# Stick-breaking attention with a woven output projection: value products sent for two steps at a time

## The chip, the cores and the metric

One core of a Trainium2 chip runs the whole program in one launch. The metric is device time in microseconds (us), the median of several runs of the same kernel. A profiled execution is a run of its own; its trace gives times from the start of its span.

## What is computed

One layer of a streaming encoder: an input projection, stick-breaking attention with 8 heads of 64 (2,048 new frames, and 8 running streams with 16 frames each over 1,024 cached ones), an HGRN2 recurrence with 4 heads of 128, an output projection and a LayerNorm. The parts that matter here, cut from the reference:

```python
def stick_breaking_attention(q, k, v, q_offset):
    z = jnp.einsum('bhqd,bhkd->bhqk', qblk, kf) * scale
    mask = kpos[None, :] < qpos[:, None]
    log_keep = jnp.where(mask, jax.nn.log_sigmoid(-z), 0.0)
    later = lax.cumsum(log_keep, axis=3, reverse=True) - log_keep
    w = jnp.where(mask, jnp.exp(jax.nn.log_sigmoid(z) + later), 0.0)
    return jnp.einsum('bhqk,bhkd->bhqd', w, vf)
...
    mixed = jnp.concatenate([o_sb, o_hg], axis=-1).astype(x.dtype)
    out = jnp.einsum('bte,ed->btd', mixed, w_out)
    y = layer_norm(DEEPNORM_ALPHA * x + out, ln_g, ln_b)
```

So per head: scores, two sigmoids of them (the weight and what is kept), a running product along the keys, and the product with the values.

## The kernel before

The program has three stages on one timeline. First come the input projection and the HGRN2 chunks (to about 1,000 us). Then the attention over the prompt runs in 160 **units**, and a second stream of work is woven between them. Last comes what is left of the output projection.

A unit is one pair of heads, one block of 128 queries and up to 512 keys (`CW`); 64 query blocks times head pairs are cut into 160 units, from the last keys to the first. The first unit of a block holds the diagonal and is 1 to 4 blocks of 128 keys wide, all others are 4 wide. A unit goes through four parts, written in `run_steps` (L1000) as a software pipeline over steps n:

- `z_part(n + 3)`, L721: the scores of both heads, one PSUM bank each (`pz`, two banks in all). Each matmul has 64 rows, and the two heads sit on the two halves of the array (L734). In the first unit of a block a mask product (L731) goes ahead of them. ScalarE then makes `s` (L737) and `keep` (L740) from the scores. For units below 90 the `keep` of the second head is made by GpSimd from `s` instead (L742).
- `s_part(n + 2)`, L746: VectorE scans `keep` (L701) and GpSimd multiplies `s` by the result (L754).
- `t_part(n)`, L759: four transposes per head (L767) into one of two PSUM banks (`pw`), copied by ScalarE to `wh` (L107).
- `c_part(n - 1)`, L771: the value products (L783). They use 64 columns of the array per head and add up over the units of a block in one PSUM bank, `po`. After the last unit of a block VectorE multiplies them with the gate (L795), and after every second block a DMA stores the result to `mx_d`.

Within a step the order on TensorE is written out by hand:

```python
for i in range(2):
    run_later(); s_part(n + LS, i)
    if 0 <= n < NU: t_part(n, i)
    if i == 1:
        z_part(n + LZ); c_part(n - 1)
    tick()
    credit[0] += rate
    while credit[0] >= 1: next(guest, None); credit[0] -= 1
```

So a step is: transposes of head 0, guest, transposes of head 1, scores, value products, guest. The **guest** is a generator that sends one piece of other work each time it is called. For steps 0 to 89 it is the attention of the running streams (`all_samples`, L971). From step 90 on it is the output projection (`out_proj`, L1161, `out_first`, L1120), called 0.9 times per half step (`ORATE`). One of its pieces is two of the eight `e`, with three matmuls each of 512 columns (`py`, L1109 to L1111), so 6 matmuls. A 128-row block takes 48. A call can also find nothing to send: where the block's inputs are not there yet, where they are being split into two parts (L1104), or where a piece of the LayerNorm's tail is run. What the guest has not sent when the units end is sent afterwards without a break. TensorE takes its instructions in this order, and each engine waits on the others by semaphores.

Of the kernel before, what the change touches and what calls it, by code (L numbers as in the profile page):

```python
# [17 lines left out]
P = 128  # L18
# [10 lines left out]
LEVELS = (1, 2, 4, 8, 16, 32, 64)  # L29
BLK = 32  # L30
C0 = -2
W0 = 6
WL = 3
I0 = 2
PRE = 2
# [30 lines left out]
def stream_step_kernel(ctx: ExitStack, tc: tile.TileContext, x_prompt, x_sample, cache_k, cache_v, state_s,  # L66
# [83 lines left out]
                units.append((job, qb, lo, min(lo + CW, nk), lo + CW >= nk, lo == 0))  # L150
    NU = len(units)
    NS = 90
    SH0 = pool
    SH1 = dve
    KE = pool
# [517 lines left out]
    with ExitStack() as ph:  # L673
# [2 lines left out]
        qk = E("qk", 2)  # L676
        row = E("row", 2)
        fix = E("fix")
        wtp = E("wtp", 4)
        pz = E("pz", 2, space=PSUM)  # L680
        one = []
        smp_ctx = ExitStack()
# [88 lines left out]
        def c_part(u):  # L771
            if u < 0 or u >= NU:
                return
            job, qb, lo, hi, top, bot = units[u]
            p = jobs[job][0]
            if top:
                Os[p] = pa.tile([P, 512], F32, name="po", tag="po")
            o, v, n = Os[p], Vs[job], (hi - lo) // P
            th = [WT.pop((u, a)) for a in range(2)]
            for x in range(n):  # L780
                for a in range(2):
                    r = slice(a * DH, (a + 1) * DH)
                    mm(o[r, :P], v[:, lo // P + x, r], th[a][:, x * P:(x + 1) * P],  # L783
                       start=top and x == 0, stop=bot and x == n - 1)
            if bot:
                finish(p, qb)

        mos = {}

        def finish(p, qb):  # L790
            po, gt, e = Os.pop(p), Gs[(p, qb // 4)], qb % 2
            if e == 0:
                mos[p] = qk.tile([P, 2, P], F32, name="mo", tag="mo", bufs=3)
            mo = mos[p]
            later.append(lambda: dve.tensor_tensor(mo[:, e], po[:, :P], gt[:, qb % 4 * P:(qb % 4 + 1) * P], ALU.mult))  # L795

            def store():
                dma.dma_start(mx_d[p][:, (qb - 1) * P:(qb + 1) * P], mo)
                done.add((p, qb // 2))

            if e:
                defer(store, 4)
# [197 lines left out]
        def run_steps(n0, n1, guest, rate):  # L1000
            for n in range(n0, n1):
                for fn in todo.pop(n, []):
                    fn()
                for i in range(2):
                    run_later()
                    s_part(n + LS, i)
                    if 0 <= n < NU:
                        t_part(n, i)
                    if i == 1:
                        z_part(n + LZ)  # L1010
                        c_part(n - 1)
                    tick()
                    if n >= -LZ:
                        credit[0] += rate
                    while credit[0] >= 1:
                        next(guest, None)
                        credit[0] -= 1
# [10 lines left out]
        hg_ctx.close()  # L1028
        pw = E("pw", 2, space=PSUM)
        px = E("px", 2, space=PSUM)  # L1030
        pa = E("pa", 1, space=PSUM)
        one.append(E("pone", 1, space=PSUM).tile([P, 1], F32, name="one"))
        dve.memset(one[0], 1.0)
        sk = smp_ctx.enter_context(ALLOC("sk"))
# [85 lines left out]
        def out_first():  # L1120
            raw = {}

            def load(e):
                if e < KT:
                    raw[e] = io.tile([P, DM], F32, name="wor", tag="xr", bufs=3)
                    dma.dma_start(raw[e], w_out[0, e * P:(e + 1) * P, :])

            load(0)
            out_load(0)
            load(1)  # L1130
            for _ in range(W0):
                yield
            bs = io.tile([P, 2, 6], F32, name="bs", tag="bs")
            ps = [px.tile([P, 512], F32, name="py", tag="px") for _ in range(2)]
            for i in range(2 * KT + WL):
                e, c = divmod(i, 2)
                if e < KT:
                    if c == 0:
                        load(e + 2)
                    cs = slice(c * 512, c * 512 + 512)  # L1140
                    h, l, r = (t[:, cs] for t in (woh[:, e], wol[:, e], raw[e]))
                    eng = (dve, pool)[c]
                    copy(act, h, r)
                    later.append(lambda eng=eng, h=h, l=l, r=r: eng.tensor_tensor(l, r, f32(h), ALU.subtract))
                if i in (0, 2):
                    out_split(0, i // 2)
                if e == KT:
                    out_load(1)
                    out_x(0)
                if i >= WL:  # L1150
                    e, c = divmod(i - WL, 2)
                    cs = slice(c * 512, c * 512 + 512)
                    out_mm(0, ps[c], e, cs)
                    if e == KT - 1:
                        add(0, bs, c, cs, ps[c])
                yield
            dma.dma_start(lng, ln_g.to_broadcast([P, DM]))
            dma.dma_start(lnb, ln_b.to_broadcast([P, DM]))
            tails.extend(norm(BLKS[0], L[0]["x"], bs))

        def out_proj():  # L1161
            yield from out_first()
            for k, blk in list(enumerate(BLKS))[1:]:
                while k not in L:
                    out_load(k)
                    yield
                    yield
                for hf in range(2):
                    if hf not in L[k]:
                        out_split(k, hf)  # L1170
                        yield
                out_load(k + 1)
                while tails:
                    run_tail()
                    yield
                out_x(k)
                x = L[k]["x"]
                bs = io.tile([P, 2, 6], F32, name="bs", tag="bs")
                for c in range(2):
                    cs = slice(c * 512, (c + 1) * 512)  # L1180
                    ps = px.tile([P, 512], F32, name="py", tag="px")
                    for e in range(KT):
                        out_mm(k, ps, e, cs)
                        if e % 2 == 1:
                            if c == 1 and e % 4 == 3:
                                out_split(k + 1, e // 4)
                            run_tail()
                            out_load(k + 1)
                            out_x(k + 1)
                            yield  # L1190
                    add(k, bs, c, cs, ps)
                tails.extend(norm(blk, x, bs))
            while tails:
                run_tail()
                yield
# [3 lines left out]
        def run_tail():  # L1199
            if tails:  # L1200
                tails.pop(0)()
# [5 lines left out]
        def norm(blk, x, bs):  # L1207
# [28 lines left out]
            def both():  # L1236
# [1 line left out]
                shift(h1, SH1)  # L1238

            skip = lambda: None  # L1240
            return [skip, stats, skip, skip, lambda: center(h0, SH0), lambda: center(h1, SH1), both,
                    lambda: store(slice(0, DM))]

        guest = out_proj()
        run_steps(NS, NU + 1, guest, ORATE)
        run_later()
        run_later()
        run_later()
# [27 lines left out]
```

## Time and profile before

| what | value |
|---|---|
| median of 3 runs | 1751.0 us (1747.85 to 1751.8) |
| the profiled execution | 1749.85 us, of which the span is 1748.0 us |
| TensorE matmul, busy | 1707.1 us of the span (98%) |
| VectorE, ScalarE, GpSimd busy | 958.5, 701.2, 731.2 us |
| chain that ended last | 92% on TensorE |
| value products (L783) | 2,176 rows, 155.0 us busy |
| scores (L734) | 640 rows, 170.5 us busy |
| transposes (L767) | 1,088 rows, 171.5 us busy |

The profile is of one execution. Rows of matmuls overlap: the time that a group takes on TensorE is read from its start to the start of the next group, not from its length. A row of the timeline such as "x16" stands for so many instructions in a row. A float32 matmul of the scores and of the value products shows as two rows each, a transpose and a matmul of the output projection as one.

### The profile page before, as it was taken

How to read it: one execution, taken by the hardware profiler on the slowest of the kernel's cores; microseconds unless marked ns; L12 is line 12 of the kernel's file. 1: busy time of each engine (PE TensorE's matmuls, PEld its weight loads, DVE VectorE, ACT ScalarE, POOL GpSimd, SP SyncE). 2: the span in 40 equal slices, each digit the busy share in tenths (PEclk: the TensorE clock that was granted, in tenths of full speed). 3: DMA queues.
4: the chain of work that ended last, by engine and by line, in shares of the span. 5: the costliest groups of instructions: out<-in, count | busy, mean ns of one | idle time of the engine just before them, and what ended most of it. 6: DMA issues, size and time to landing. Idle time of an engine off the chain costs nothing.

```text
span 1748.0 us, 33628 instructions
## 1 busy us (share of the span) xinstructions
PE 1707.1 (98%) x12901; PEld 1464.1 (84%) x12901; DVE 958.5 (55%) x1762; ACT 701.2 (40%) x1593; POOL 731.2 (42%) x822
## 2 busy tenths in 40 slices
PE   8999999999999999999999999999999999999998
PEld 8999999999999999999999866666666667666886
DVE  4254543355443352642665367777877767666454
ACT  3221220212213222211222267777777877767210
POOL 1122321213221322221222266666766776766564
PEclk9999999999999999999999989999999999999999
DMA  4133232122244231231122476786644533131243
GB/s 166 53 89 102 63 100 61 48 63 62 81 120 135 62 103 56 80 90 40 61 62 76 124 189 159 176 187 152 152 113 136 185 114 102 53 114 40 92 147 115
DMA packets 288167, 180.01 MB, mean 103 GB/s; under 512 B 112636, under 2 KB 272904, under 8 KB 288008
## 3 DMA queue, kind: packets, MB, share of 16 engines
q1 hardware_dynamic: 288008, 177.86, 35.9%
q8 instruction: 103, 1.69, 0.4%
q14 instruction: 56, 0.46, 0.1%
HBM read 130.63 MB, written 47.71 MB: 102 GB/s over the span
## 4 chain that ended last, share of the span: by engine, by line
PE 92%; DVE 3%; ACT 1%; DMA 1%; issue 1%; SPq 1%; POOL 0%; POOLq 0%; DVEq 0%; ACTq 0%
PE pj L309 11%; PE pj L311 10%; PE pj L310 10%; PE z L734 9%; PE po L783 7%; PE wt L767 7%; PE py L1109 4%; PE ps L418 4%; PE pj L319 4%; PE pj L321 4%; PE pj L320 4%; PE py L1111 4%; PE py L1110 4%; PE pk L864 2%; PE so L945 1%; PE ps L431 1%
## 5 line engine op out<-in xcount | busy, mean ns | idle before, releaser
L115 POOL TENSOR_TENSOR wl<-wr,wh 128x512 fp32r<-128x512 f32 x126 | 163.8, 1322 | 578.7 <-ACT wh L107 561.0
L309 PE MATMUL pj<-xh,wh 128*128 128x384 f32 (+1 forms) x1152 | 395.5, 343 | 0.0
L754 POOL TENSOR_TENSOR s<-s,pr 128x512 f32<-128x512 f32 (+3 forms) x320 | 325.7, 1024 | 130.0 <-DVE pr L701 112.8
L311 PE MATMUL pj<-xh,wl 128*128 128x384 f32 (+1 forms) x1152 | 376.2, 327 | 0.0
L310 PE MATMUL pj<-xl,wh 128*128 128x384 f32 (+1 forms) x1152 | 375.8, 326 | 0.0
L701 DVE TENSOR_TENSOR_SCAN pr<-keep,pr,one 128x513 f32<-128x513 f32 x192 | 238.7, 1270 | 74.1 <-ACT keep L740 67.5
L309 PEld LDWEIGHTS pj<-xh,wh 128*128 128x128 f32 x1152 | 217.3, 189 | 2.7 <-issue 0.7
L310 PEld LDWEIGHTS pj<-xl,wh 128*128 128x128 f32 x1152 | 217.5, 189 | 0.7 <-issue 0.7
L311 PEld LDWEIGHTS pj<-xh,wl 128*128 128x128 f32 x1152 | 216.7, 188 | 0.0
L783 PEld LDWEIGHTS po<-wh,vst 128*64 128x64 f32 x2176 | 116.3, 137 | 100.6 <-issue 82.3
L737 ACT ACTIVATE s<-z 128x512 f32<-128x512 f32 (+3 forms) x320 | 173.4, 542 | 61.4 <-PE z L734 57.8
L107 ACT COPY wh<-wt 128x512 f32<-128x512 f32 (+3 forms) x320 | 165.6, 539 | 78.2 <-PE wt L767 65.1
L767 PE MATMUL wt<-ident,s 128*128 128x128 f32 x1088 | 171.5, 282 | 0.2
L734 PE MATMUL z<-kst,qr 64*128 64x512 f32 (+3 forms) x640 | 170.5, 587 | 0.1
L767 PEld LDWEIGHTS wt<-ident,s 128*128 128x128 f32 x1088 | 124.0, 142 | 45.2 <-issue 19.1
L319 PE MATMUL pj<-wh,xh 128*128 128x256 f32 x544 | 160.4, 295 | 0.0
L783 PE MATMUL po<-wh,vst 128*64 128x128 f32 x2176 | 155.0, 281 | 0.0
L320 PE MATMUL pj<-wl,xh 128*128 128x256 f32 x544 | 152.3, 280 | 0.3 <-POOL wl L115 0.3
L321 PE MATMUL pj<-wh,xl 128*128 128x256 f32 x544 | 152.2, 280 | 0.0
L327 ACT ACTIVATE sg<-pj 128x384 f32<-128x384 f32 (+1 forms) x72 | 34.1, 474 | 231.3 <-PE pj L311 217.9
L740 ACT ACTIVATE keep<-z 128x512 f32<-128x512 f32 (+2 forms) x230 | 126.0, 548 | 0.0
L701 DVE TENSOR_TENSOR_SCAN pr<-keep,one 128x385 f32<-128x385 f32 (+3 forms) x124 | 99.7, 820 | 33.2 <-ACT keep L740 17.6
(162 smaller groups left out, 2783.8 us busy)
## 6 DMA issues: line engine op xcount, KB each, us to landing
wr<-in_w_in SPq DMA_DIRECT2D x64, 512.0 KB
kr<-in_cache_k SPq DMA_DIRECT2D x16, 1024.0 KB
vr<-in_cache_v SPq DMA_DIRECT2D x32, 512.0 KB
mt<-mx_d SPq DMA_DIRECT2D x136, 64.0 KB
x<-in_x_prompt SPq DMA_DIRECT2D x16, 512.0 KB
kst<-kT_d SPq DMA_DIRECT2D x16, 512.0 KB
vst<-v_d SPq DMA_DIRECT2D x16, 512.0 KB
out<-xr SPq DMA_DIRECT2D x16, 512.0 KB
```

What stands on the lines that cost most here:

```text
L309: mm(o, wh[:, k], xh[:, k, :n], start=k == 0, stop=False)
L310: mm(o, wh[:, k], xl[:, k, :n], start=False, stop=False)
L311: mm(o, wl[:, k], xh[:, k, :n], start=False, stop=k == KT - 1)
L319: mm(o, xh[:, k, ts], wh[:, k], start=k == 0, stop=False)
L320: mm(o, xh[:, k, ts], wl[:, k], start=False, stop=False)
L321: mm(o, xl[:, k, ts], wh[:, k], start=False, stop=k == KT - 1)
L701: dve.tensor_tensor_scan(pr[:, CW - wd:CW + 1][:, ::-1], kr, by, carry, ALU.mult, ALU.bypass)
L734: mm(z[:, :wd], q[r, q0:q0 + P], k[r, lo:hi], start=not top, stop=True, skip_group_check=True)
L737: act.activation(s[:, :wd], z[:, :wd], AF.Sigmoid, scale=SC)
L754: pool.tensor_tensor(s[:, :wd], s[:, :wd], pr[:, CW - wd + 1:CW + 1], ALU.mult)
L767: nc.tensor.transpose(pt_[:, x:x + P], U[(u, a)][0][:, x:x + P], ident)
L783: mm(o[r, :P], v[:, lo // P + x, r], th[a][:, x * P:(x + 1) * P], start=top and x == 0, stop=bot and x == n - 1)
```

## The change

Value products are sent for two units at once, behind the scores of every even step (`CB = 2`), and in the odd steps none. `po` is now one PSUM bank with four slots of 128 columns, taken in turn, where a block's sums had a tile of their own from a pool of one bank. `wh` has eight buffers instead of four. The output projection's piece is four of the eight `e` (12 matmuls) instead of two, and its guest is called half as often; `W0`, the LayerNorm's list of tail calls and the calls of `run_tail` are recast for the longer pieces.

```diff
-W0 = 6
+W0 = 3
...
+    CB = 2
...
-        wtp = E("wtp", 4)
+        wtp = E("wtp", 8)
...
             if top:
-                Os[p] = pa.tile([P, 512], F32, name="po", tag="po")
-            o, v, n = Os[p], Vs[job], (hi - lo) // P
-            th = [WT.pop((u, a)) for a in range(2)]
+                slot[0] += 1
+            o, v, n = po[:, slot[0] % 4], Vs[job], (hi - lo) // P
+            th = [WT.pop((u, a), None) for a in range(2)]
+            if th[0] is None:
+                return
             for x in range(n):
                 for a in range(2):
                     r = slice(a * DH, (a + 1) * DH)
-                    mm(o[r, :P], v[:, lo // P + x, r], th[a][:, x * P:(x + 1) * P],
-                       start=top and x == 0, stop=bot and x == n - 1)
+                    mm(o[r], v[:, lo // P + x, r], th[a][:, x * P:(x + 1) * P],
+                       start=top and x == 0, stop=bot and x == n - 1, skip_group_check=True)
             if bot:
-                finish(p, qb)
+                finish(p, qb, o)
...
                     if i == 1:
                         z_part(n + LZ)
-                        c_part(n - 1)
+                        if n % CB == 0 or n >= NU:
+                            for c in range(n - CB, n):
+                                c_part(c)
...
-        pa = E("pa", 1, space=PSUM)
+        po = E("pa", 1, space=PSUM).tile([P, 4, P], F32, name="po")
...
-                yield
+                if i % 2:
+                    yield
+            yield
...
-                        if e % 2 == 1:
-                            if c == 1 and e % 4 == 3:
+                        if e % 4 == 3:
+                            if c == 1:
                                 out_split(k + 1, e // 4)
+                            run_tail()
                             run_tail()
...
-            return [skip, stats, skip, skip, lambda: center(h0, SH0), lambda: center(h1, SH1), both,
+            return [skip, skip, stats, skip, lambda: center(h0, SH0), lambda: center(h1, SH1), both,
...
-        run_steps(NS, NU + 1, guest, ORATE)
+        run_steps(NS, NU + 1, guest, ORATE / 2)
```

Counted over TensorE's whole order, the value products stood in 159 groups and now stand in 80. The 816 matmuls of the output projection stood in 64 pieces between steps, and 480 of them behind the last value products. Now 25 pieces stand between steps and 576 matmuls behind the end.

Two places show it. The first is TensorE at the block of queries 14 of the last head pair, where the guest has nothing to send (`z` are scores, `po` value products, `wt` transposes; an instruction of `z` or `po` here is two rows in the trace). Before:

```order
L731 MATMUL z<-ntri,identr 128x128 x2
L734 MATMUL z<-kst,qr 128x384 x2
L783 MATMUL po<-wh,vst 64x128 x4
L767 MATMUL wt<-ident,s 128x128 x8
L734 MATMUL z<-kst,qr 128x512 x2
L783 MATMUL po<-wh,vst 64x128 x8
L767 MATMUL wt<-ident,s 128x128 x8
L734 MATMUL z<-kst,qr 128x512 x2
L783 MATMUL po<-wh,vst 64x128 x8
L767 MATMUL wt<-ident,s 128x128 x6
L734 MATMUL z<-kst,qr 128x512 x2
L783 MATMUL po<-wh,vst 64x128 x8
```

And with the change, at the same units:

```order
L732 MATMUL z<-ntri,identr 128x128 x2
L735 MATMUL z<-kst,qr 128x384 x2
L768 MATMUL wt<-ident,s 128x128 x8
L735 MATMUL z<-kst,qr 128x512 x2
L786 MATMUL po<-wh,vst 64x128 x12
L768 MATMUL wt<-ident,s 128x128 x8
L735 MATMUL z<-kst,qr 128x512 x2
L768 MATMUL wt<-ident,s 128x128 x6
L735 MATMUL z<-kst,qr 128x512 x2
L786 MATMUL po<-wh,vst 64x128 x16
```

Between every other two scores only the transposes are left.

The second place is TensorE one block further on, where the output projection (`py`) is sent between steps. Before:

```order
L783 MATMUL po<-wh,vst 64x128 x6
L1109 MATMUL py<-woh,mh 128x512
L1110 MATMUL py<-wol,mh 128x512
L1111 MATMUL py<-woh,ml 128x512
L1109 MATMUL py<-woh,mh 128x512
L1110 MATMUL py<-wol,mh 128x512
L1111 MATMUL py<-woh,ml 128x512
L767 MATMUL wt<-ident,s 128x128 x4
```

And with the change (the last six of twelve, and what follows):

```order
L1115 MATMUL py<-woh,mh 128x512
L1116 MATMUL py<-wol,mh 128x512
L1117 MATMUL py<-woh,ml 128x512
L1115 MATMUL py<-woh,mh 128x512
L1116 MATMUL py<-wol,mh 128x512
L1117 MATMUL py<-woh,ml 128x512
L768 MATMUL wt<-ident,s 128x128 x8
L735 MATMUL z<-kst,qr 128x512 x2
L786 MATMUL po<-wh,vst 64x128 x16
```

A step now has one long piece or none, where it had two short ones or none.

## Rows read from the trace of the kernel before

**Rows 1.** The page: busy time of TensorE, and its granted clock in 40 slices.
```profile
PE 1707.1 (98%) x12901; PEld 1464.1 (84%) x12901; DVE 958.5 (55%) x1762; ACT 701.2 (40%) x1593; POOL 731.2 (42%) x822
...
PEclk9999999999999999999999989999999999999999
```
**Rows 2.** Busy time by stretch: span, each engine's busy us, granted clock, DMA.
```profile
1012.00:1354.00 342.00, 331.36 (x3294) 223.37 (x3295) 258.81 (x316) 260.99 (x585) 232.97 (x292) 1.00 0.65 158
1354.00:1630.00 276.00, 275.25 (x2068) 190.65 (x2068) 189.44 (x208) 203.12 (x419) 186.74 (x180) 1.00 0.31 99
```
**Rows 3.** Timeline of TensorE, steps without guest: start, us, instruction, count.
```profile
1589.30 0.66 PE L783 MATMUL po<-wh,vst 128*64 128x128 f32 x8
1589.88 1.09 PE L767 MATMUL wt<-ident,s 128*128 128x128 f32 x8
1590.90 1.36 PE L734 MATMUL z<-kst,qr 64*128 64x512 f32 x4
1592.20 1.09 PE L783 MATMUL po<-wh,vst 128*64 128x128 f32 x16
...
1594.24 1.13 PE L734 MATMUL z<-kst,qr 64*128 64x512 f32 x4
1595.30 1.09 PE L783 MATMUL po<-wh,vst 128*64 128x128 f32 x16
1596.33 0.87 PE L767 MATMUL wt<-ident,s 128*128 128x128 f32 x6
1597.13 1.57 PE L734 MATMUL z<-kst,qr 64*128 64x512 f32 x4
1598.63 1.09 PE L783 MATMUL po<-wh,vst 128*64 128x128 f32 x16
```
**Rows 4.** Timeline of ScalarE, same steps: first and last of four operations.
```profile
1595.46 0.60 ACT L737 ACTIVATE s<-z 128x512 f32<-128x512 f32 x1 [0.31 <-PE z L734]
...
1596.91 0.62 ACT L740 ACTIVATE keep<-z 128x512 f32<-128x512 f32 x1
```
**Rows 5.** Timeline of TensorE's weight loads, same steps, second head's scores.
```profile
1597.58 0.29 PEld L734 LDWEIGHTS z<-kst,qr 64*128 64x128 f32 x2 [0.15 <-ACT keep L740]
```
**Rows 6.** Timeline of TensorE, scores of two steps below unit 90.
```profile
1028.62 1.13 PE L734 MATMUL z<-kst,qr 64*128 64x512 f32 x4
...
1031.07 1.52 PE L734 MATMUL z<-kst,qr 64*128 64x512 f32 x4
```
**Rows 7.** Waits of the weight loads, 1354 to 1630 us: us in total, times, longest.
```profile
PEld z L734 <- ACT keep L740: 3.5, 15, 0.7
...
PEld z L731 <- ACT keep L740: 1.1, 3, 0.7
PEld z L734 <- ACT s L737: 1.0, 6, 0.2
```
**Rows 8.** Timeline of TensorE, the last two units' value products, sent together.
```profile
1628.55 1.97 PE L783 MATMUL po<-wh,vst 128*64 128x128 f32 x32
1630.45 0.50 PE L1109 MATMUL py<-woh,mh 128*128 128x512 f32 x1
```
**Rows 9.** Timeline of TensorE, a piece of the output projection between transposes.
```profile
1508.89 0.60 PE L767 MATMUL wt<-ident,s 128*128 128x128 f32 x4
1509.25 0.48 PE L1109 MATMUL py<-woh,mh 128*128 128x512 f32 x1
1509.57 0.40 PE L1110 MATMUL py<-wol,mh 128*128 128x512 f32 x1
...
1510.72 0.60 PE L767 MATMUL wt<-ident,s 128*128 128x128 f32 x4
1511.25 1.13 PE L734 MATMUL z<-kst,qr 64*128 64x512 f32 x4
```
**Rows 10.** Busy time by stretch, as in rows 2, at the first units.
```profile
990.00:998.00 8.00, 5.95 (x43) 5.07 (x41) 1.84 (x4) 2.11 (x8) 1.51 (x7) 0.99 0.23 72
998.00:1012.00 14.00, 13.43 (x47) 6.86 (x48) 7.21 (x10) 6.29 (x19) 8.20 (x16) 0.52 0.89 209
```

More of the change, by code (lines that the diff above doesn't have):

```diff
@@ L782, in c_part, with finish @@
                     r = slice(a * DH, (a + 1) * DH)
-                    mm(o[r, :P], v[:, lo // P + x, r], th[a][:, x * P:(x + 1) * P],
-                       start=top and x == 0, stop=bot and x == n - 1)
+                    mm(o[r], v[:, lo // P + x, r], th[a][:, x * P:(x + 1) * P],
+                       start=top and x == 0, stop=bot and x == n - 1, skip_group_check=True)
             if bot:
-                finish(p, qb)
+                finish(p, qb, o)
         mos = {}
-        def finish(p, qb):
-            po, gt, e = Os.pop(p), Gs[(p, qb // 4)], qb % 2
+        slot = [0]
+        def finish(p, qb, o):
+            gt, e = Gs[(p, qb // 4)], qb % 2
             if e == 0:
@@ L794, in finish @@
             mo = mos[p]
-            later.append(lambda: dve.tensor_tensor(mo[:, e], po[:, :P], gt[:, qb % 4 * P:(qb % 4 + 1) * P], ALU.mult))
+            later.append(lambda: dve.tensor_tensor(mo[:, e], o, gt[:, qb % 4 * P:(qb % 4 + 1) * P], ALU.mult))
             def store():
```

## Prediction

> **What bounds the kernel now.** I read the page first. TensorE is busy for 98% of the span, at full clock almost throughout [rows 1]. So time is won or lost where TensorE changes what it does or waits for somebody. The busy time by stretch narrows it to the units: from 1012 to 1354 us (guest: the running streams) and from 1354 to 1630 us (guest: the output projection). There TensorE is busy for 331 of 342 and 275 of 276 us [rows 2]. ScalarE is busy for 261 of 342 and 203 of 276 us, about 75%; it is the one to look at next, because the scores have only two PSUM banks, one per head, and ScalarE must have read both before the next scores may be written.
>
> The timelines show that loop. In steps without guest, scores begin at 1594.24 and ScalarE's four operations on them run from 1595.46 to 1597.53. Scores of the second head start at 1597.58, with ScalarE's `keep` named as the one they waited for, 3.34 us after the scores before [rows 3 to 5]. TensorE had been ready at 1597.13; the scores row is 1.57 us long in place of 1.13, and the value products start at 1598.63, not at 1598.19. So **from full scores to the next second head there are at least 3.34 us**, if ScalarE makes four operations (units from 90). With three (below 90) it is 2.84: scores at 1028.62, and the next at 1031.07 plus 1.52 less 1.13 [rows 6].
>
> In between TensorE does, from start to start: scores 1.06 (1594.24 to 1595.30), value products 1.03, transposes 1.02 for eight and 0.80 for six [rows 3]. That is 3.11 us against 3.34, nearly even. The kernel before therefore waits little: 3.5, 1.1 and 1.0 us in the later stretch [rows 7], and by three lengthened scores like that of 1031.07 [rows 6] about 1.0 in the earlier one, 6.6 us in all.
>
> **The change, part by part.** *Merged value products.* 79 of 159 groups go. The last two units of the kernel before already send theirs together: 32 rows take 1.90 us, from 1628.55 to 1630.45 [rows 8], where two groups take 2 x 1.03 = 2.06. That is 0.16 us per merge, and 79 x 0.16 = 12.6 us. No row at full clock has scores followed directly by transposes, which is what stands in every odd step now, so the price has bounds. The lower one is 0, if this change of array shape costs all that the group's entry cost. The upper one is 0.16 + 0.17 = 0.33: four transposes take 0.36 before `py`, which has their shape, and 0.53 before scores, which have not [rows 9], and this 0.17 may go as well. I take 0.16, the only measured merge. The Trainium skill, TensorEngine Tiling (Array Packing), section Key Properties, says that changing the tiling mode drains TensorE. By that rule three changes stand in each old step and five in two new ones, one drain less per pair; it gives no price, and with the upper bound as its price the sum is that of the first rival.
>
> *Longer pieces of the output projection.* Its first matmul takes 0.32 us, the five after it 1.15, or 0.23 each [rows 9]: 0.09 per piece. 64 pieces between steps become 25: 39 x 0.09 = 3.5 us saved. The 96 matmuls that move behind the last unit cost nothing by themselves, 0.23 us each here or there. What they covered in the steps is counted next.
>
> *The new wait.* In every other step the value products no longer stand between two scores. With no guest TensorE is ready for the next scores 1.06 + 1.02 = 2.08 us after the last ones, but the second head must wait until 3.34. That is a wait of **1.26 us**, and behind it, in order, stand the value products of two units and the transposes. The first head alone may go at about 2.36 (its `keep` ends two operations, about 1.0 us, earlier), which helps nothing: 1597.58 + 1.05 = 1598.63 shows that the value products come 1.05 after the second head's start [rows 3, 5]. In the other step of the pair the merged products make 4 us out of 3.1, more than the loop needs, and what is over there cannot be handed on.
>
> I counted the steps of the new order that have neither value products nor guest. From step 91 on there are 20. Fifteen follow full scores: eight with eight transposes wait 1.26, four with six wait 1.48, one with four 1.70, two with two 1.92 (transposes taken at 0.11 us each, as eight differ from six). That is 10.1 + 5.9 + 1.7 + 3.8 = 21.5 us. Five follow narrower scores; I estimate 2.0 for them, and 0.5 for two steps with a short guest. Below step 91, with 2.84, seven steps behind full scores wait 0.2 to 1.4, 6.2 us together, and three narrower ones 1.5. Sum: 24.0 + 7.7 = 31.7 us, in place of 6.6: **25.1 us lost**.
>
> The bounds of this term are wide. If the first head's release at 2.36 were all that counts, it would be some 11 us in place of 31.7, and the loss 4.4. If ScalarE's splits of the guest (L1104, two operations per block, 0.6 us each if as long as those of rows 4) fall into the loop, five blocks add up to 6 us.
>
> *The rest at nothing.* The gate's product on VectorE no longer stands before the next block's sums, but it had a step's time and shows no wait worth a row. The stores to `mx_d` go out up to one step later on the DMA queue; the guest that needs them has the tail behind it, where TensorE works without a break. The eight `wh` buffers only let the first unit's copies live longer. `W0`, the tail's list and the doubled `run_tail` keep the old pace in time. If the tail ran dry, one missed block would cost its 48 x 0.23 = 11 us, but 576 matmuls now stand there.
>
> **Sum.** 25.1 - 12.6 - 3.5 = +9.0 us. Against the profiled execution's 1749.85 us that gives 1758.85; the median of the runs lies 1.15 above that execution, so **1760.0 us**. A difference of 0.2%, 3.5 us, is what a measurement of this kernel can tell from none.
>
> **Rivals.** *First: the change of array shape is worth more than the waits.* Place: the transposes behind scores in the odd steps. At the upper price of 0.33 the merges give 26.1 us, with the pieces 29.6, and the sum is 25.1 - 29.6 = -4.5: **1746.5 us, faster**. It decides from (25.1 - 3.5) / 79 = 0.27 us per merge. For it: the 0.17 before scores is real. Against it: the one merge that the trace shows gave 0.16, and in a step that waits for ScalarE a cheaper switch only lengthens the wait. If the second head did not wait for its own bank, but only for the first, it would come out at 1749.85 + 1.15 + 4.4 - 16.1 = 1739.3; the row at 1597.58 speaks against that. Chance 0.18.
>
> *Second: no difference.* A price between 0.23 and 0.31, or waits a third shorter than counted, leaves less than 3.5 us either way: about 1751. For it: the two large terms are of the same size and opposite sign. Chance 0.18.
>
> *Third: the clock falls.* From 990 to 998 us TensorE was busy for 5.95 of 8 us, with gaps between scores that waited for `keep`; from 998 to 1012 the granted clock was 0.52, the 1.2 GHz level [rows 10]. A run of guestless steps after the change has gaps of the same origin: steps 104 to 115 are twelve in a row. At half clock a pair's 6.1 us of work takes 12.2 instead of the 7.3 with its wait, 4.9 more; six pairs lose 29 us: 1789 us. Against it: the first head's scores, which may start at 2.36, fill most of each gap. The Trainium skill, TensorE: Matmul & The Clock Gate, section HAM oscillation — how this bites in real kernels, says that a wait long enough between bursts brings the half rate back each time; the drop at 998 agrees. Chance 0.05.
>
> That the change does not do what it says is ruled out by TensorE's order: 80 groups and 25 pieces stand there.
>
> **How the numbers follow.** The forecast has 0.59; with its waits off by a tenth (3.2 us) and the price of a merge by a quarter (3.2 us) it covers 1754 to 1766. With the third rival that makes 0.64 for slower, 0.18 for the same, 0.18 for faster. The range goes from 1745, which takes in the first rival at its upper price, to 1772, which takes in merges that save nothing (1760.0 + 12.6 = 1772.6) all but a rest; the clock and the 1739 of the lower bound are left out.
>
> **What would show it.** Right: in the trace after, scores behind which only transposes stood are about 2.1 us long where they were 1.13, because the first head starts at about 2.36 and the second at 3.34; waits of score weight loads for `keep` several times those of before; merged products of 32 rows 1.90 us from start to start; the stretch to the last value products longer by about 9 us less 22 us (96 x 0.23) and the tail longer by 22. Wrong: scores directly behind transposes with the second head starting less than 3.3 us after the scores before; a transposes group behind scores that starts well under 1.06 us after them; a granted clock under full in a guestless stretch; or the total of waits for `keep` unchanged.

## The result and the profile after

The changed kernel takes **1766.1 us** (median of 4 runs, 1764.23 to 1767.86) beside 1749.42 us of the kernel before on the same chip: ratio 1.0094, 95% interval 1.0078 to 1.0109. It is slower by 16.7 us; 1760.0 was predicted, in the range of 1745 to 1772. The profiled execution's span went from 1748.0 to 1763.8 us.

The page of the changed kernel: span, busy time, granted clock, and the group of the scores (busy us, mean ns | idle time before them and who ended it).

```profile
span 1763.8 us, 33341 instructions
...
PE 1706.1 (97%) x12901; PEld 1468.1 (83%) x12901; DVE 956.2 (54%) x1762; ACT 696.2 (39%) x1593; POOL 732.8 (42%) x822
...
PEclk9999999999999999999999999999999999999999
...
L735 PE MATMUL z<-kst,qr 64*128 64x512 f32 (+3 forms) x640 | 182.6, 584 | 7.3 <-ACT keep L741 7.2
```

The same group in the page of the kernel before:

```profile
L734 PE MATMUL z<-kst,qr 64*128 64x512 f32 (+3 forms) x640 | 170.5, 587 | 0.1
```

TensorE has as many matmuls as before and is busy 1 us less [rows 1], while the span grew by 15.8. The scores alone took 12.1 us more of busy time and 7.2 us more of idle time: waits are partly hidden inside "busy", because a group of four score matmuls whose second half waits counts as one long row. The clock is near full in every slice. It was at half for part of the first units, as in the kernel before, but for a shorter part (0.52 there [rows 10]; the third number from the right is the granted clock):

```profile
998.00:1012.00 14.00, 12.55 (x68) 7.06 (x65) 8.47 (x13) 8.10 (x23) 9.54 (x19) 0.76 0.94 224
```

Busy time by stretch, same bounds and columns as [rows 2]:

```profile
1012.00:1354.00 342.00, 322.08 (x3219) 220.10 (x3217) 253.63 (x312) 253.68 (x573) 228.97 (x288) 1.00 0.64 156
1354.00:1630.00 276.00, 269.81 (x2064) 185.58 (x2063) 182.13 (x198) 201.76 (x423) 179.65 (x172) 1.00 0.28 90
```

TensorE lost 9.3 and 5.4 us of busy time in the two stretches, and every other engine was busy less as well. Nobody became the bound; a loop between two engines did. The timeline of TensorE shows one pair of steps without guest (start, us, instruction, count; in brackets idle time and its releaser):

```profile
1402.24 1.97 PE L786 MATMUL po<-wh,vst 128*64 128x128 f32 x32
1404.14 1.09 PE L768 MATMUL wt<-ident,s 128*128 128x128 f32 x8
...
1405.34 1.13 PE L735 MATMUL z<-kst,qr 64*128 64x512 f32 x4
1406.40 1.10 PE L768 MATMUL wt<-ident,s 128*128 128x128 f32 x8
1407.70 2.10 PE L735 MATMUL z<-kst,qr 64*128 64x512 f32 x4 [0.20 <-ACT keep L741]
1409.73 1.75 PE L786 MATMUL po<-wh,vst 128*64 128x128 f32 x28
```

The weight loads of the scores at 1407.70, and the first and last of ScalarE's four operations on the scores of 1405.34:

```profile
1407.69 0.29 PEld L735 LDWEIGHTS z<-kst,qr 64*128 64x128 f32 x2 [0.43 <-ACT keep L741]
1408.67 0.29 PEld L735 LDWEIGHTS z<-kst,qr 64*128 64x128 f32 x2 [0.69 <-ACT keep L741]
```
```profile
1406.56 0.60 ACT L738 ACTIVATE s<-z 128x512 f32<-128x512 f32 x1 [0.65 <-PE z L735]
...
1408.01 0.62 ACT L741 ACTIVATE keep<-z 128x512 f32<-128x512 f32 x1
```

This is the predicted picture almost to the digit. The first head's scores come 2.36 us after the scores before (1405.34 to 1407.70), the second head's 3.33 (1408.67), and the row is 2.10 us long where a free one is 1.13. The merged products behind it start at 1409.73. From step 91 on there are 15 such rows, each of 2.10 us, as many as the steps counted behind full scores. The total, by the waits of the weight loads from 1350 to 1625 us (us, times, longest):

```profile
PEld z L735 <- ACT keep L741: 21.9, 40, 1.1
```

Before it was 3.5 us in 15 waits [rows 7]. The stretch with the running streams brings something that the prediction does not have. The waits of TensorE's matmuls from 1005 to 1350 us, after and before:

```profile
PE pk L868 <- ACT om L960: 8.5, 6, 1.7
PE pk L868 <- DVE ms__10167 L969: 3.0, 5, 1.2
```
```profile
PE pk L864 <- ACT om L956: 5.1, 6, 1.3
...
PE pk L864 <- DVE ms__10166 L965: 1.2, 2, 1.0
```

`pk` are the streams' key transposes, `om` the copy of a finished stream's output out of a PSUM bank that `pk` needs next, and `ms_` the gated output. These waits grew by 3.4 + 1.8 = 5.2 us. One of them, in TensorE's timeline after and before:

```profile
1199.86 1.13 PE L735 MATMUL z<-kst,qr 64*128 64x512 f32 x4
1200.92 0.55 PE L768 MATMUL wt<-ident,s 128*128 128x128 f32 x3
...
1203.25 0.66 PE L868 MATMUL pk<-ident,kr 128*128 128x128 f32 x4 [1.68 <-ACT om L960]
```
```profile
1200.40 1.13 PE L734 MATMUL z<-kst,qr 64*128 64x512 f32 x4
1201.46 1.09 PE L783 MATMUL po<-wh,vst 128*64 128x128 f32 x16
1202.49 0.55 PE L767 MATMUL wt<-ident,s 128*128 128x128 f32 x3
...
1203.82 0.66 PE L864 MATMUL pk<-ident,kr 128*128 128x128 f32 x4 [0.68 <-ACT om L956]
```

From scores to `pk` it is 3.39 us after and 3.42 before. The value products' 1.03 us stood inside a wait for ScalarE, which in the changed kernel copies `om` at 1202.89, behind three passes over the scores of 1199.86 and one copy to `wh`; with the products gone, the wait is 1.00 us longer.

To place the time, I use four marks: the first scores, the scores of unit 93 and of unit 159 (the last), and the end. "Residual waits" are the spacing of the scores of two steps less the work that stands between them, counted from start-to-start times at full clock (scores 1.06, value products 0.15 + 0.11 each, transposes 0.11, matmuls of the output projection 0.09 + 0.23 each, the streams' work likewise). Their zero is arbitrary, since the streams' work is counted roughly, so only their difference from the kernel before is shown: steps 12 to 89, and 90 on.

| profiled kernel | first scores | to unit 93 | to unit 159 | to the end | residual 12 to 89 | residual 90 on | clock 998 to 1012 us |
|---|---|---|---|---|---|---|---|
| before | 995.20 | 347.07 | 274.75 | 131.0 | 0 | 0 | 0.52 |
| after | 996.12 | 349.94 | 260.09 | 157.6 | +12.1 | +20.5 | 0.76 |
| e1, products of one step | 995.53 | 344.43 | 250.49 | 157.2 | 0.0 | +5.5 | 0.76 |
| e2, short pieces | 998.48 | 350.38 | 281.69 | 131.9 | +12.2 | +12.4 | 0.76 |
| e3, keep on GpSimd | 998.38 | 353.18 | 253.29 | 157.4 | +13.5 | +13.3 | 0.60 |
| e5, products twice | 995.50 | 347.92 | 260.06 | 157.6 | +12.0 | +6.1 | 1.00 |
| e6, sent at turnovers | 995.53 | 346.06 | 259.27 | 158.0 | +5.3 | +20.1 | 0.76 |
| e7, held beside guest | 995.55 | 343.28 | 270.24 | 132.2 | +1.8 | -0.2 | 0.63 |
| e9, list of e7 amended | 997.44 | 344.41 | 270.57 | 132.2 | +1.7 | 0.0 | 0.57 |
| e10, e7 with long pieces | 995.70 | 344.45 | 248.00 | 158.0 | +1.7 | +6.1 | 0.51 |

With the long pieces 114 matmuls of the output projection (612 instead of 498) stand behind the last scores, 114 x 0.2275 = 25.9 us that leave the third column for the fourth. The first scores come between 995.2 and 998.5, although the work ahead of them is the same; this is why the stretches are compared and not the spans alone. The three late ones, e2, e3 and e9, lost most of it at 540 us: TensorE waited there for a load of `x` (1.95 us in e2, 1.65 in the kernel before), and the granted clock from 541 to 545 us was then 0.60, 0.70 and 0.82, and 1.00 in the kernel before.

The first twelve steps are left out of the residuals, which are 9 to 13 us there by run: they wait for the loads of the streams' caches, and part of them runs at half clock. The last column tells the runs apart. From the first scores to those of unit 8 it is 25.66 us in the kernel before (clock 0.52), 23.19 in the changed one and 23.14 in e1 (0.76 both), and 21.22 in e5 (1.00). So 2 to 4 us between two profiles can be this clock and no effect of the order.

### The profile page after: what moved, and what is told of

Read it like the earlier page. It is cut to its first block, busy times and chain, and to the rows that moved or that the text cites. A ratio compares the mean times of both kernels' runs of the same rounds, so it can differ in the third digit from the quotient of the medians.

```text
span 1763.8 us, 33341 instructions
## 1 busy us (share of the span) xinstructions
PE 1706.1 (97%) x12901; PEld 1468.1 (83%) x12901; DVE 956.2 (54%) x1762; ACT 696.2 (39%) x1593; POOL 732.8 (42%) x822
## 4 chain that ended last, share of the span: by engine, by line
PE 90%; DVE 4%; ACT 2%; issue 2%; DMA 2%; POOL 1%; SPq 0%; POOLq 0%; DVEq 0%; ACTq 0%
PE pj L310 11%; PE pj L312 10%; PE pj L311 10%; PE z L735 9%; PE po L786 7%; PE wt L768 6%; PE ps L419 4%; PE pj L320 4%; PE py L1115 4%; PE pj L322 4%; PE pj L321 4%; PE py L1117 4%; PE py L1116 3%; PE pk L868 2%; PE ps L432 1%
## 5 line engine op out<-in xcount | busy, mean ns | idle before, releaser
L755 POOL TENSOR_TENSOR s<-s,pr 128x512 f32<-128x512 f32 (+3 forms) x320 | 323.0, 1014 | 142.1 <-DVE pr L702 117.6
L702 DVE TENSOR_TENSOR_SCAN pr<-keep,pr,one 128x513 f32<-128x513 f32 x192 | 238.5, 1270 | 67.4 <-ACT keep L741 56.4
L735 PE MATMUL z<-kst,qr 64*128 64x512 f32 (+3 forms) x640 | 182.6, 584 | 7.3 <-ACT keep L741 7.2
L768 PE MATMUL wt<-ident,s 128*128 128x128 f32 x1088 | 167.6, 282 | 0.5 <-POOL s L755 0.3
L786 PE MATMUL po<-wh,vst 128*64 128x128 f32 x2176 | 136.4, 276 | 0.0
```

Of the source, the lines that this page charges most:

```text
L702: dve.tensor_tensor_scan(pr[:, CW - wd:CW + 1][:, ::-1], kr, by, carry, ALU.mult, ALU.bypass)
L735: mm(z[:, :wd], q[r, q0:q0 + P], k[r, lo:hi], start=not top, stop=True, skip_group_check=True)
L755: pool.tensor_tensor(s[:, :wd], s[:, :wd], pr[:, CW - wd + 1:CW + 1], ALU.mult)
L768: nc.tensor.transpose(pt_[:, x:x + P], U[(u, a)][0][:, x:x + P], ident)
L786: mm(o[r], v[:, lo // P + x, r], th[a][:, x * P:(x + 1) * P], start=top and x == 0, stop=bot and x == n - 1, skip_group_check=True)
```

## The experiments

All medians stand beside runs of the kernel before on the same chip; the ratio is to these.

### e1: products of one step each, long pieces kept

```diff
-    CB = 2
+    CB = 1
```

> The changed kernel with one edit: value products go out after every step's scores again (159 groups), the long pieces of the output projection, the four slots and the eight copies stay. Theory (the second head's scores wait for ScalarE's last reading of their bank because no value products stand between): the waits of score weight loads for keep after 1350 us fall from 21.9 us to 9 or less, no scores row is 2.10 us long, and the time is that of the kernel before, 1749.4, less 3.5 for the pieces, plus 0.24 for each of 16 more guestless steps behind full scores: 1750, within 3. Rival (the long pieces starve the steps between them): the time stays above 1760.

Measured: 1751.95 us, ratio 1.0012 (1.0002 to 1.0023). As expected; the loss comes from merging. The waits for `keep` are 3.8 us, and no scores row behind step 91 is longer than 1.92 us. By the counts of the table, long pieces alone cost 5.5 us of residual waits in the later steps and save 3.9 (250.49 + 25.9 - 274.75 = +1.65, less 5.5). The waits follow from 15 more steps without guest: 20 steps from 90 on have 0.3 to 0.8 us each though their products stand in place; before there were 10.

### e2: merged products, short pieces as before

```diff
-W0 = 3
+W0 = 6
...
-                if i % 2:
-                    yield
-            yield
+                yield
...
-                        if e % 4 == 3:
-                            if c == 1:
+                        if e % 2 == 1:
+                            if c == 1 and e % 4 == 3:
...
-        run_steps(NS, NU + 1, guest, ORATE / 2)
+        run_steps(NS, NU + 1, guest, ORATE)
```

> The changed kernel with the output projection's short pieces of before (6 matmuls, called twice as often, the old list of tail calls, W0 = 6); the merged value products stay. Steps behind full scores that have neither products nor guest fall from 15 to 9 after step 91. Theory: nine waits of about 1.4 us instead of fifteen, the earlier stretch as in the changed kernel: 1749.4 + 2.9 (first stretch, as measured) - 34 x 0.16 + 14.5 - 5.6 = 1756, within 3. Rival (long pieces are the cause): 1750 or less.

Measured: 1763.38 us, ratio 1.0076 (1.0061 to 1.0091). Missed by 7 us, on the side of the theory: the rival is out. Of the miss, 3.3 us stand before the first scores, where nothing was changed and where the clock fell as told above. The later steps cost 12.4 us where 14.5 - 5.6 = 8.9 were counted. Of the difference, 1.7 us are the clock again: behind the wait of one guestless pair it fell to half, and 32 rows of merged products took 3.56 us in place of 1.90. The timeline, and the granted clock of that stretch (third number from the right):

```profile
1572.88 2.10 PE L735 MATMUL z<-kst,qr 64*128 64x512 f32 x4 [0.86 <-ACT keep L741]
1574.91 3.63 PE L786 MATMUL po<-wh,vst 128*64 128x128 f32 x32
1578.47 0.66 PE L768 MATMUL wt<-ident,s 128*128 128x128 f32 x4
```
```profile
1574.90:1578.50 3.60, 3.60 (x34) 3.26 (x33) 1.88 (x2) 1.26 (x3) 3.60 (x4) 0.53 0.31 118
```

In the steps beside the streams merging alone costs 12.2 us, as much as in the changed kernel. Against 79 x 0.16 = 12.6 us saved, 12.2 and 12.4 are a net loss of 12 us. The 12.2 beside the streams, nearly twice the 6.7 counted there, asked for e6.

### e3: the second head's keep always on GpSimd

```diff
-                if a == 0 or u >= NS:
+                if a == 0:
```

> The changed kernel with one edit: the keep of the second head is made by GpSimd from s in all units, as it is below unit 90. ScalarE then has three operations on the scores instead of four. Theory: the second head may start 2.84 us after the scores before instead of 3.34, so each of the 15 waits falls by 0.5 us and scores rows are about 1.6 us long instead of 2.10: 1766 - 8 = 1758, within 3. Rival (the wait is not this loop): no change; or GpSimd, about 65% busy in that stretch, becomes the bound and the time rises.

Measured: 1759.19 us, ratio 1.0057 (1.0043 to 1.0072). As expected: 6.9 us less than the changed kernel (6.5 by the ratios), all in the later steps (260.09 to 253.29). The 15 scores rows of 2.10 us are 1.61 us long. With one ScalarE pass fewer in the loop, the waits of the scores' weight loads for `keep` fall from 21.9 to 9.1 us. The wait is ScalarE's time over the scores, and not something of TensorE's own. The 1.4 us more beside the streams (13.5 against 12.1) fit the clock, 0.51 from 1209 to 1212.5 us in this profile, behind a wait of 1.68 us for `om`.

### e4 and e8: a third score bank, and its control

e4 gives the scores a third PSUM bank; the bank is taken from `one`, the single column that is the scan's second operand, which moves to SBUF. e8 moves `one` alone. `new_z`, not shown here, takes every third scores tile from the new bank.

```diff
-            zs = [pz.tile([P, CW], F32, name="z", tag="pz") for _ in range(2)]
+            zs = [new_z() for _ in range(2)]
...
-        one.append(E("pone", 1, space=PSUM).tile([P, 1], F32, name="one"))
+        zb.append(E("pz3", 1, space=PSUM))
+        one.append(fix.tile([P, 1], F32, name="one"))
```

> The changed kernel with three PSUM banks for scores, used in turn by the heads; the third comes from moving the one-column constant of the scan from PSUM to SBUF. The second head then waits for the first head's bank of the step before, free 2.36 us after those scores began, where TensorE is ready at 2.08. Theory: the waits fall from 1.26 to about 0.3 us per guestless pair, and the merges keep their 0.16 each: 1766 less 18 to 23 = 1743 to 1748, at or under the kernel before. Rival (the loss is not the banks): 1760 or more; a slower scan from SBUF would show in VectorE's row.

Measured: 1863.3 us, ratio 1.0647 (1.0631 to 1.0663): missed by over 115 us. The scores did stop waiting for `keep`, 2.1 us in 5 waits from 1350 to 1700 us, but TensorE now waited for GpSimd. The groups of the scan, of GpSimd's multiply and of the transposes' weight loads in e4's page:

```profile
L763 POOL TENSOR_TENSOR s<-s,pr 128x512 f32<-128x512 f32 (+3 forms) x320 | 436.8, 1377 | 120.1 <-DVE pr L702 97.8
...
L702 DVE TENSOR_TENSOR_SCAN pr<-keep,pr,one 128x513 f32<-128x513 f32 x192 | 328.9, 1735 | 51.9 <-POOL keep L751 27.5
...
L776 PEld LDWEIGHTS wt<-ident,s 128*128 128x128 f32 x1088 | 123.5, 145 | 127.8 <-POOL s L763 86.7
```

The first two groups in the changed kernel, with `one` in PSUM:

```profile
L755 POOL TENSOR_TENSOR s<-s,pr 128x512 f32<-128x512 f32 (+3 forms) x320 | 323.0, 1014 | 142.1 <-DVE pr L702 117.6
...
L702 DVE TENSOR_TENSOR_SCAN pr<-keep,pr,one 128x513 f32<-128x513 f32 x192 | 238.5, 1270 | 67.4 <-ACT keep L741 56.4
```

> The changed kernel with one thing moved: the single column that is the scan's second operand lies in SBUF instead of PSUM, two score banks as ever. It is the control for the run with three banks. If the operand's place made that run slow: about 1861 +-15, scans of 128x513 at about 1735 ns against 1270, GpSimd's multiplies near 1.7 us. Rival (the third bank's own order cost it): about 1766 with scans at 1270 ns.

Measured: 1865.26 us, ratio 1.0645 (1.0625 to 1.0665). The control alone costs all of it, and its scans are as slow:

```profile
L702 DVE TENSOR_TENSOR_SCAN pr<-keep,pr,one 128x513 f32<-128x513 f32 x192 | 333.4, 1760 | 47.6 <-POOL keep L743 27.9
```

The slow scans are among those that GpSimd works beside. Of e8's 240 scans of 128x513, the 11 with no GpSimd instruction beside them took 1.22 to 1.29 us; the other 229 took 1.77 on average. Two of them, the first alone, the second beside the GpSimd multiply that is shown under it:

```profile
1551.89 1.27 DVE L702 TENSOR_TENSOR_SCAN pr<-keep,pr,one 128x513 f32<-128x513 f32 x1
...
1553.26 2.15 DVE L702 TENSOR_TENSOR_SCAN pr<-keep,pr,one 128x513 f32<-128x513 f32 x1
```
```profile
1553.24 1.09 POOL L755 TENSOR_TENSOR s<-s,pr 128x512 f32<-128x512 f32 x1 [1.40 <-DVE pr L702]
```

So e4 tells nothing about the time of a third bank. It shows only that with three banks most waits for `keep` go: 2.1 us, and 12.7 us in 25 waits in the control over the same window. Part of the loss of both runs can be the clock: from 1050 to 1640 us 0.93 was granted in e4 and 0.94 in e8, where single waits for GpSimd are up to 3.9 and 3.2 us long; how much it cost isn't shown. Whether a third bank would pay with `one` still in PSUM wasn't tried: the kernel's pools hold eight banks, and the third score bank took the place of `one`.

### e5: the empty steps filled with products that nobody reads

```diff
+        def spare(u):
...
+                    mm(o[r], v[:, lo // P + x, r], WT[(u, a)][:, x * P:(x + 1) * P],
...
+                        if n + 1 in SPARE:
+                            spare(n - 1)
```

`SPARE` lists the 15 steps. `spare` writes to the slot after next, `po[:, (slot[0] + 2) % 4]`. The starting matmuls there also restart the sums of the block that is open in the same bank, so this kernel's attention output lacks part of them. (So the Trainium skill has it, PSUM — Partial Sum Buffer, section PSUM: the matmul accumulator: two groups open in one bank cannot both begin with a clearing matmul. No time rests on it.)

> The changed kernel (1766.1) with more work: at the 15 steps behind full scores that have neither products nor guest work, the newest unit's value products are sent once more, into a slot whose sums are never read. By the counts of the order that is 10 x 8 and 5 x 6 matmuls, 10 x 1.03 + 5 x 0.81 = 14.4 us of TensorE. Theory (TensorE stands there for about 1.25 us a pair of steps anyway, for the two keep passes): 1766 to 1769. Rival (the empty steps cost nothing, the loss comes from elsewhere): 1766.1 + 14.4 = 1780.5.

Measured: 1768.36 us beside 1752.32 of the kernel before, ratio 1.0087 (1.0071 to 1.0103), against 1.0094 of the changed kernel. **14.4 us of TensorE work cost nothing.** The later stretch is 260.06 us long with it and 260.09 without. The pair of steps of above, in this kernel's timeline (the extra products are the 12 records at 1403.79):

```profile
1402.73 1.13 PE L736 MATMUL z<-kst,qr 64*128 64x512 f32 x4
1403.79 0.88 PE L798 MATMUL po<-wh,vst 128*64 128x128 f32 x12
1404.59 1.09 PE L769 MATMUL wt<-ident,s 128*128 128x128 f32 x8
1405.62 1.57 PE L736 MATMUL z<-kst,qr 64*128 64x512 f32 x4
1407.12 1.75 PE L787 MATMUL po<-wh,vst 128*64 128x128 f32 x28
...
1409.82 1.13 PE L736 MATMUL z<-kst,qr 64*128 64x512 f32 x4
```

From scores to the second scores after them it is 7.09 us, and 7.09 in the changed kernel (1405.34 to 1412.43). The scores in the middle start at 2.89 us in place of 2.36 (the extra products took 0.80) and are 1.57 us long in place of 2.10; the merged products behind them come at the same distance, 4.39 us.

### e6: products sent at once where the streams hand over a bank

```diff
-                        if n % CB == 0 or n >= NU:
-                            for c in range(n - CB, n):
+                        pend.append(n - 1)
+                        if n + 1 not in HOLD or n >= NU:
+                            for c in pend:
                                 c_part(c)
+                            pend.clear()
```

`HOLD` has the even steps without the 16 turnovers; e7, e9 and e10 differ in this list.

> The changed kernel (1766.1), but at the 16 steps where the running streams hand over a bank (their transposes of one 128-wide product block or of the copied output, lines L917 and L963 of the guest) the pending products are sent at once, so these pairs aren't merged. Theory (the first stretch rose by the streams' own waits, which the products had covered: residual waits on these steps 4.5 and 3.1 us more than before): -7.6 + 15 x 0.16 = -5.2, 1761 +-2, the length of the first stretch down from 349.9 to about 345, pk waits on om back near 5 us. Rival (the first stretch rose for something else): only the merges are lost, 1768.5.

Measured: 1762.91 us beside 1752.32, ratio 1.0062 (1.0049 to 1.0075). As expected: 0.0032 below the changed kernel, 5.6 us, though 15 merges are given up. The residual of the first stretch falls from +12.1 to +5.3, its length to 346.06, and the waits for `om` are back to the size they had before:

```profile
PE pk L868 <- ACT om L960: 4.9, 6, 1.3
```

So more than half of what the first stretch lost stood at these turnovers.

### e7: products held only beside guest work

Short pieces as before the change; `HOLD` has the 52 steps whose guest work, or whose narrow scores, leave no gap (by the rows of the kernels before and after).

> Half-long pieces as before the change, and products held over a step only where that step has guest work enough or narrow scores ahead of it (52 steps by a fixed list), sent at once everywhere else. Theory (a saved group is worth 0.16 us and costs nothing where other work stands in its place): 1749.9 - 52 x 0.16 = 1741.6, range 1740 to 1745, waits of z on keep as before (3 to 4 us). Rival (holding products back costs something wherever it is done): 1748 or more.

Measured: 1745.24 us beside 1752.32, ratio **0.9963 (0.9950 to 0.9976)**: faster than both kernels. The kernel before ran 2.4 us higher beside these runs, so 1745.24 lies just outside the expected range; by the ratio the gain is 6.5 us of the 8.3 expected. Its page, the waits of its weight loads from 1350 to 1610 us, and two steps of it:

```profile
span 1741.3 us, 33329 instructions
...
L735 PE MATMUL z<-kst,qr 64*128 64x512 f32 (+3 forms) x640 | 168.6, 585 | 0.0
```
```profile
PEld z L735 <- ACT keep L741: 2.7, 12, 0.6
```
```profile
1407.05 0.66 PE L768 MATMUL wt<-ident,s 128*128 128x128 f32 x4
1407.46 0.49 PE L1118 MATMUL py<-woh,mh 128*128 128x512 f32 x1
...
1408.95 0.60 PE L768 MATMUL wt<-ident,s 128*128 128x128 f32 x4
...
1409.65 0.49 PE L735 MATMUL z<-kst,qr 64*128 64x128 f32 x4
1410.08 1.97 PE L786 MATMUL po<-wh,vst 128*64 128x128 f32 x32
1411.97 0.66 PE L768 MATMUL wt<-ident,s 128*128 128x128 f32 x4
```

The guest stands where the products are held back, the scores do not wait, and the merged products take 1.89 us from start to start. From the first scores to the last it is 613.5 us, and 621.8 before: 8.3 us for 52 merges, 0.16 each, or 0.17 if the small changes of the waits (+1.6, and -1.0 in the first twelve steps, where the clock was 0.63 and not 0.52) are taken out. The tail gives back 1.2 us (132.2 against 131.0).

### e9 and e10: two amendments

e9 takes the two steps with the largest residual out of e7's list and shifts the pairs behind them (51 steps). e10 is e7 with the long pieces and its own list (44 steps).

> As the run that holds products only beside guest work, with 51 steps in the list: the two with the largest residual waits there (steps 94 and 145, 1.65 and 0.81 us) are out, the pairs after them shifted by one. Theory (what is left to gain are these two waits): ratio to the kernel before about 0.995, one to two us under that run, 1743.5 +-2.5. Rival (their waits move to a neighbour): as that run, 0.9963.

Measured: 1745.7 us beside 1750.23, ratio 0.9970 (0.9959 to 0.9981), not told apart from e7's. The rival had it: step 145 keeps its 0.8 us with products in place, and step 94's wait moved to 95 (1.1).

> The changed kernel's long pieces, with products held only beside guest work (44 steps, chosen by the same rule from the order that the long pieces give). Theory (long pieces cost 2 us net, as the run with long pieces and single products showed, since 15 more steps have no guest, at some 0.3 us each, against 3.5 us saved; merges give 44 x 0.16 = 7.0): ratio 1.0012 - 0.0040 = 0.997, 1745 +-2.5. Rival (with products in place, long pieces keep their 3.5 us): 0.994 or less, 1740.

Measured: 1748.67 us, ratio 0.9990 (0.9981 to 0.9998). Both theory and rival missed, on the slow side. The later steps wait 6.1 us more than before, as in e1 (5.5), so long pieces cost here too. Of the miss of 3.5 us, 1.7 are residual waits beside the streams that e7 shows as well, 0.6 later waits (6.1 against 5.5) and 0.8 the tail (158.0 against 157.2). The first twelve steps are 2.7 us longer than in e1's profile, but that is the clock of the two profiles, 0.51 here and 0.76 in e1; in the kernel before it was 0.52. The short pieces stay.

## Why the prediction was right, and where its size was off

**The direction and its reason** hold. The loop between scores and ScalarE has the lengths of [rows 3 to 5] (3.34 us to the second head; 3.33 found), the guestless steps wait in it (scores of 2.10 us), and e3 and e5 show that the time is ScalarE's: with a pass fewer the loss shrinks by 6.9 us (6.5 by the ratios), and 14.4 us of work fit into it for nothing.

**The merge at 0.16 us** holds. Rows of 32 took 1.90 us (1402.24 to 1404.14), as in [rows 8]. Transposes directly behind scores started 1.06 us after them, as value products do, so the 0.17 of the first rival is not there; e7's 8.3 us for 52 merges confirms the price. That rival, which needed 0.27, is out. The second, no difference, is out by the interval.

**The pieces at -3.5 us** hold as a saving (3.9 by e1, where it is what is left beside the counted waits). What they uncover was counted with the waits.

**The waits** are the term that was mis-sized. The prediction counted +25.1 us; the residuals give +30.6 over all steps (+12.1 and +20.5, less 2.0 in the first twelve steps, where the clock of the two profiles differed). From step 91 on the count was 24.0 - 5.6 = 18.4 and the trace has 20.5. Below it the count was 7.7 - 1.0 = 6.7 and the trace has 12.1. The sentence that failed is "Below step 91 ... seven steps behind full scores wait ... 6.2 us together": it asked only of the score loop who waits when the value products leave. The streams' own matmuls wait for ScalarE and VectorE as well, for a PSUM bank to be emptied, and the products had stood inside these waits too. Their rows, 5.1 and 1.2 us, were in the trace of before, with no group among the rows read. They grew by 5.2 us, which is the missing 5.4, and e6 took it back by putting products at these places again.

By spans: +9.0 predicted, +5.4 and +2.1 in the waits, -2.0 in the first twelve steps, +0.9 before the first scores and +0.7 behind the last make 16.1; 15.8 was measured. The -2.0 is chance, the clock of two single executions in the first units, and makes the miss look smaller.

**The clock** (third rival) did not fall in the changed kernel's guestless steps: 1.00 in both stretches, with waits of up to 1.1 us once per pair. In [rows 10] TensorE was idle for 2.05 of the 8 us ahead of the drop; a guestless pair here has 1.25 of 7.09. But the rival's mechanism occurs: in e2's profile the clock fell once behind a guestless pair and cost 1.7 us, and in e3's once behind the wait for `om`. The rule of the Trainium skill cited with that rival agrees with these two places. The same waits, 0.86 us idle ahead of the scores (at 1427.70 and 1490.47) and 1.68 ahead of `pk`, left the clock at 1.00 in the changed kernel's profile, so a wait of this size brings the half rate at times and not each time; what decides is not shown here. The rival's 29 us were seen nowhere.

**The rest at nothing** (gate's product, stores, `wh` buffers, tail) shows no row that speaks against it: the tail is 157.6 us, 131.0 + 25.9 + 0.7.

## What to carry to other kernels

Before work is moved off a place, ask of every wait near it, and not only of the loop that one has in mind, how long it would be without that work: a wait of 0.7 us in the trace may be one of 1.7 with 1 us of cover. Merging saves its 0.16 us only where something else stands in the gap, so the merges are chosen step by step and not by parity: 52 chosen ones gain 6.5 us where 79 in every second step, with the same short pieces, lose 13 (e2). And an unread copy of the work, put back into the gap, is a cheap proof of whether the gap is free.

## What was not expected of the hardware

Moving one column, the scan's second operand, from PSUM to SBUF made the whole kernel 5.5% slower (1.0645 in e8 against 1.0094 in the changed kernel). VectorE's scan of 128x513 went from 1270 to 1760 ns, and GpSimd's multiply from 1014 to 1370 ns on average. The Trainium skill, SBUF — State Buffer, section Who interferes with whom, says that a VectorE instruction with two SBUF inputs contends with a GpSimd instruction that reads SBUF, and that one with at most one SBUF input, outside the modes that use two ports, does not. The runs agree: `keep` was in SBUF already, and `one` made it two. With no GpSimd instruction beside it a scan of e8 took 1.27 us, as in the changed kernel, and beside a multiply 2.15.
